# Stick-breaking attention: the break probabilities stay in PSUM and are scanned there

## The chip, the core and the metric

The kernel runs on one core of a Trainium2 chip. The metric is the device time of one execution in microseconds (us). TensorE (PE in the profile) multiplies matrices and writes PSUM, which has eight banks of 128 x 512 fp32 values here; ScalarE (ACT) evaluates functions, VectorE (DVE) does elementwise work and scans, GpSimd (POOL) does elementwise work on SBUF, and SyncE (SP) issues the transfers.

## What is computed

One inference step of a two-layer encoder: 2048 prompt rows and 64 sample rows, each layer with four groups of heads. Group C, which the change touches, is stick-breaking attention, strictly causal, four heads of 64:

```python
z = jnp.einsum('bqhd,bkhd->bhqk', q, k).astype(jnp.float32) * Dh ** -0.5
mask = kpos[None, :] < qpos[:, None]
log_1m = jnp.where(mask, jax.nn.log_sigmoid(-z), 0.0)
tail = lax.cumsum(log_1m, axis=3, reverse=True) - log_1m
w = jnp.where(mask, jnp.exp(jax.nn.log_sigmoid(z) + tail), 0.0)
return jnp.einsum('bhqk,bkhd->bqhd', w.astype(v.dtype), v)
```

So the weight of a key is sigmoid(z) times the product of sigmoid(-z) over all later keys. The kernel works with the products themselves, not with logarithms. Groups A (band attention with a bias), B (latent attention) and M (memory tokens) are softmax attention. A large projection goes into every layer and another comes out of it.

## The kernel before

Two streams of work are written into one program. The projection stream (`p_stream`) multiplies row tiles of 128 by weights that are split into a high and a low part (POOL at line 304, DVE at line 305, tile `wh`) and sums three matmuls for each of eight slices into the PSUM tile `pp` (lines 402, 403, 405). The attention stream (`attention`) walks over units; a unit is up to two query tiles against at most four key tiles. A planner (`target`) chooses after every few instructions which of the two streams goes on. The program that results is then ordered for each engine by a scheduler, which works through the instructions by the place at which they were written and by its own estimate of when their inputs are ready; each engine executes its instructions strictly in that order.

A unit u passes through stages that are spread over several turns of the loop: the scores (`step`, once for each query tile), then `s1b`; a turn later the transposes of its weights (`s2`, PSUM tile `pt`, line 900, with the split into `ph` by ACT at line 903 and DVE at line 136); a turn after that the products with the values (`s3`, line 925). For group C the class is `Stick`. One step: two score matmuls into the PSUM tile `ps` (lines 855, 856), on the diagonal a mask added by DVE (line 1090), sigmoid(-z) by ACT into the SBUF tile `cc` (line 1093), sigmoid(z) by ACT into the SBUF tile `s` (line 1094). In `s1b`, for each of the unit's one or two query tiles: the carry of the later keys is copied (line 1109) or set to one (line 1107), DVE scans `cc` from right to left into `r` (line 1110), and POOL multiplies `s` by `r` (line 1113). A scan's two tensor inputs are both `cc`: the second stands in a minimum that never binds.

The tiles `ps`, `pt` and those of the projection stream's transposes share five PSUM banks (pool `ps_st`). `cc` shares its four SBUF buffers with the keys `kr` of group B; `r` has three buffers, `s` four.

Of the kernel before, what the change touches and what calls it, by code (L numbers as in the profile page):

```python
# [7 lines left out]
F32 = mybir.dt.float32  # L8
F32R = mybir.dt.float32r
BF16 = mybir.dt.bfloat16  # L10
ACTF = mybir.ActivationFunctionType
ALU = mybir.AluOpType
# [52 lines left out]
def hybrid_step(  # L65
# [15 lines left out]
    V, A, G, T = nc.vector, nc.scalar, nc.gpsimd, nc.tensor  # L81
# [5 lines left out]
    def pool(name, bufs=1, **kw):  # L87
        return ctx.enter_context(tc.tile_pool(name=name, bufs=bufs, **kw))

    const = pool("const")  # L90
# [3 lines left out]
    at = pool("at")  # L94
# [22 lines left out]

    mhalf = const.tile([128, 32], F32, name="mhalf")
    V.memset(mhalf, -0.5)

    NQ = 3
    qbuf = [const.tile([128, 2, 256], F32R, name=f"qbuf{i}") for i in range(NQ)]
# [729 lines left out]
    def scores(ps, q, qr, i, kt, kr, c0, n):  # L852
        w = n * 128
        qs = slice(i * 128, (i + 1) * 128)
        T.matmul(ps[:, 0:w], lhsT=q[:, 0, qs], rhs=kt[:, c0:c0 + w], start=True, stop=False)  # L855
        T.matmul(ps[:, 0:w], lhsT=q[:, 1, qs], rhs=kt[:, c0:c0 + w], start=False, stop=(qr is None))  # L856
        if qr is not None:
            T.matmul(ps[:, 0:w], lhsT=qr[:, qs], rhs=kr[:, c0:c0 + w], start=False, stop=True)

    def s_tile():  # L860
        return at.tile([128, 640], F32, tag="s", name="s", bufs=4)
# [87 lines left out]
    class Whole(Unit):  # L949
        def s1a(self):  # L950
            self.sb, self.ps = [], []
            p = self.pair
            for i, (a, e) in enumerate(self.ranges):
                self.sb.append(s_tile())
                for c in sorted({j // 4 for j in range(a, e)}):
                    self.ps.append((i, c))
            self.mx = at.tile([128, 2, 2], F32, tag="mx", name="mx", bufs=4)
            self.k = 0
# [4 lines left out]
        def step(self):  # L963
            p = self.pair
            i, c = self.ps[self.k]
            a, e = self.ranges[i]
            j0, j1 = max(a, 4 * c), min(e, 4 * c + 4)
            w = (j1 - j0) * 128
            ps = ps_st.tile([128, 512], F32, name="ps")
            scores(ps, p["q"], None, i, p["kv"][c][:, 0], None, (j0 - 4 * c) * 128, j1 - j0)  # L970
            o0 = (j0 - a) * 128
            out = self.sb[i][:, o0:o0 + w]
            m = 0 if c == a // 4 else 1
            mx = self.mx[:, i, m:m + 1]
            if self.g == "M":
                V.tensor_scalar(out=out, in0=ps[:, 0:w], scalar1=1.0, scalar2=None, op0=ALU.mult, op1=ALU.max,
                                accum_out=mx)
            else:
                off = j0 * 128 if p["sample"] else 640 - (e - j0) * 128
                V.tensor_tensor_reduce(out=out, in0=ps[:, 0:w], in1=p["bt"][:, off:off + w], scale=1.0,  # L980
                                       scalar=-3e38, op0=ALU.add, op1=ALU.max, accum_out=mx)
            self.k += 1

        def s1b(self):
            p, n = self.pair, self.n
            nm = at.tile([128, 2], F32, tag="nm", name="nm", bufs=6)
            two = [a // 4 != (e - 1) // 4 for a, e in self.ranges]
            V.tensor_scalar(out=nm[:, 0:n], in0=self.mx[:, 0:n, 0], scalar1=-1.0, scalar2=None, op0=ALU.mult)
            if all(two):
                V.scalar_tensor_tensor(out=nm[:, 0:n], in0=self.mx[:, 0:n, 1], scalar=-1.0, in1=nm[:, 0:n],  # L990
                                       op0=ALU.mult, op1=ALU.min)
            else:
                for i in range(n):
                    if two[i]:
                        V.scalar_tensor_tensor(out=nm[:, i:i + 1], in0=self.mx[:, i, 1:2], scalar=-1.0,
                                               in1=nm[:, i:i + 1], op0=ALU.mult, op1=ALU.min)
            for i, (a, e) in enumerate(self.ranges):
                w = (e - a) * 128
                A.activation(out=self.sb[i][:, 0:w], in_=self.sb[i][:, 0:w], func=ACTF.Exp, bias=nm[:, i:i + 1],
                             accum_out=p["rspark"][:, p["qi"][i], p["h"]:p["h"] + 1])  # L1000
# [68 lines left out]

    class Stick(Unit):  # L1070
        def s1a(self):
            self.sb, self.cc, self.k = [], [], 0

        def more(self):
            return self.k < self.n
# [1 line left out]
        def step(self):  # L1077
            p, i = self.pair, self.k
            a, e = self.ranges[i]
            c = a // 4  # L1080
            w = (e - a) * 128
            ps = ps_st.tile([128, 512], F32, name="ps")
            mask = None
            if p["sample"]:
                mask = tri[:, 1]
            elif e == p["ends"][i]:
                mask = tri[:, 0]
            scores(ps, p["q"], None, i, p["kv"][c][:, 0], None, 0, e - a)
            if mask is not None:
                V.tensor_tensor(out=ps[:, w - 128:w], in0=ps[:, w - 128:w], in1=mask, op=ALU.add)  # L1090
            s = s_tile()
            cc = at.tile([128, 512], F32, tag="kr", name="cc", bufs=4)
            A.activation(out=cc[:, 0:w], in_=ps[:, 0:w], func=ACTF.Sigmoid, scale=-0.125)  # L1093
            A.activation(out=s[:, 0:w], in_=ps[:, 0:w], func=ACTF.Sigmoid, scale=0.125)
            self.sb.append(s)
            self.cc.append(cc)
            self.k += 1

        def s1b(self):
            p = self.pair  # L1100
            carry = p.setdefault("carry", [None, None])
            for i, (a, e) in enumerate(self.ranges):
                w = (e - a) * 128
                s, cc = self.sb[i], self.cc[i]
                r = at.tile([128, 513], F32, tag="r", name="r", bufs=3)
                if carry[i] is None:
                    G.memset(r[:, w:w + 1], 1.0)
                else:
                    V.tensor_copy(r[:, w:w + 1], carry[i][:, 0:1])
                V.tensor_tensor_scan(r[:, 0:w][:, ::-1], cc[:, 0:w][:, ::-1], cc[:, 0:w][:, ::-1], r[:, w:w + 1],  # L1110
                                     ALU.mult, ALU.min)
                carry[i] = r
                G.tensor_tensor(out=s[:, 0:w], in0=s[:, 0:w], in1=r[:, 1:w + 1], op=ALU.mult)  # L1113

    def load_kv(d, g, h, c, n, sample):
        kv = at.tile([128, 2, 512], F32R, tag="kv", name="kv", bufs=5)
# [321 lines left out]
    def target(x):  # L1438
        for (x0, y0), (x1, y1) in zip(knots, knots[1:]):
            if x <= x1:  # L1440
                return y0 + (y1 - y0) * (x - x0) / (x1 - x0)
        return knots[-1][1]
# [5 lines left out]
    while gens:  # L1448
# [8 lines left out]
        if len(free) == 2:  # L1457
            s = "a" if at_pos["p"] >= target(at_pos["a"]) else "p"
        else:
            s = free[0]  # L1460
# [110 lines left out]
```

## Time and profile before

| what | value |
|---|---|
| median of 3 runs | 3382.83 us (3377.99 to 3388.35) |
| the profiled execution | 3392.03 us |
| its span, first to last instruction | 3390.2 us |
| PE busy | 3177.9 us, 94% |
| DVE busy | 2728.9 us, 80% |
| ACT busy | 1939.0 us, 57% |
| POOL busy | 1598.4 us, 47% |
| granted TensorE clock, mean | 0.985 |

The profile is one execution seen by the hardware profiler. Each engine has a row of busy time; matmuls are pipelined and overlap, so a busy PE is not a PE at its peak. The idle time before an instruction is put down to the engine whose signal came last. 1.8 us of the profiled execution's time lie outside its span.

### The profile page before, as it was taken

The numbers are of one execution on the slowest core, as the hardware profiler recorded it, in microseconds if no ns is written. First come the engines' busy times: TensorE is split into PE (matmuls) and PEld (weight loads), VectorE is DVE, ScalarE is ACT, GpSimd is POOL, SyncE is SP. The second block draws the span as 40 slices with busy tenths as digits, with TensorE's granted clock in tenths as the row PEclk, the third lists the DMA queues.
The fourth block names the chain that finished last, engine by engine and source line by source line (L and its number), as shares of the span: only waits on it lengthen the run. The fifth ranks groups of instructions, "written<-read, shape, count | busy, mean of one in ns | idle before, by whom it ended". The sixth has DMA issues, their size and how long they took to land. (4 is left out here: it accounts for less than half of the span.)

```text
span 3390.2 us, 75857 instructions
## 1 busy us (share of the span) xinstructions
PE 3177.9 (94%) x24486; PEld 3029.8 (89%) x24486; DVE 2728.9 (80%) x7976; ACT 1939.0 (57%) x5336; POOL 1598.4 (47%) x2353
## 2 busy tenths in 40 slices
PE   8999899899999998999999899988999999999898
PEld 7899899789999988999999788978898998888898
DVE  5686777999788789887778977899878888776994
ACT  4455655567665555566556665656646566654651
POOL 4564455666344256542434635477424454112563
PEclk9999999999999998999999999999999999999999
DMA  6555776435656656565566567634455766556534
GB/s 198 168 147 165 205 203 191 131 101 155 172 155 192 194 165 166 141 191 154 145 186 193 146 177 209 194 111 118 140 142 160 207 193 192 151 149 179 153 110 147
DMA packets 576123, 558.95 MB, mean 165 GB/s; under 512 B 70960, under 2 KB 478000, under 8 KB 575728
## 3 DMA queue, kind: packets, MB, share of 16 engines
q1 hardware_dynamic: 575728, 554.10, 58.3%
q8 instruction: 196, 3.21, 0.4%
q14 instruction: 199, 1.63, 0.2%
HBM read 378.21 MB, written 173.75 MB: 163 GB/s over the span
## 5 line engine op out<-in xcount | busy, mean ns | idle before, releaser
L403 PE MATMUL pp<-wh,xh 128*128 128x256 f32 x4416 | 1268.4, 291 | 33.6 <-DVE wh L305 32.3
L402 PE MATMUL pp<-wh,xh 128*128 128x256 f32 x4416 | 1259.8, 290 | 21.9 <-ACT ev L437 14.4
L405 PE MATMUL pp<-wh,xl 128*128 128x256 f32 (+1 forms) x4416 | 1250.5, 285 | 0.6 <-DVE xl L136 0.4
L403 PEld LDWEIGHTS pp<-wh,xh 128*128 128x128 f32 x4416 | 839.9, 191 | 64.0 <-DVE wh L305 51.3
L402 PEld LDWEIGHTS pp<-wh,xh 128*128 128x128 f32 x4416 | 837.5, 191 | 39.2 <-ACT ev L437 18.5
L405 PEld LDWEIGHTS pp<-wh,xl 128*128 128x128 f32 x4416 | 845.1, 192 | 9.3 <-DVE xl L136 0.8
L304 POOL TENSOR_SCALAR wh<-raw,gc 128x256 fp32r<-128x256 f32 (+1 forms) x848 | 500.1, 604 | 301.6 <-PE pp L405 146.3
L925 PE MATMUL ot<-ph,kv 128*128 128x256 f32 (+1 forms) x3104 | 591.8, 294 | 34.3 <-DVE ph L136 18.8
L903 ACT CAST ph<-pt 128x512 fp32r<-128x512 f32 (+2 forms) x840 | 451.0, 551 | 259.6 <-PE pt L900 231.0
L136 DVE TENSOR_TENSOR ph<-pt,ph 128x512 fp32r<-128x512 f32 (+2 forms) x840 | 525.9, 634 | 68.7 <-ACT ph L903 64.8
L900 PE MATMUL pt<-identr,s 128*128 128x128 f32 x3056 | 509.7, 277 | 25.2 <-POOL s L1113 8.0
L925 PEld LDWEIGHTS ot<-ph,kv 128*128 128x128 f32 x3104 | 458.7, 191 | 56.5 <-DVE ph L136 28.0
L1113 POOL TENSOR_TENSOR s<-s,r 128x512 f32<-128x512 f32 (+3 forms) x328 | 359.6, 1102 | 311.4 <-DVE r L1110 136.9
L305 DVE SCALAR_TENSOR_TENSOR wh<-raw,gc,wh 128x256 fp32r<-128x256 f32 (+1 forms) x848 | 472.5, 582 | 25.0 <-POOL wh L304 22.9
L1110 DVE TENSOR_TENSOR_SCAN r<-cc,r 128x512 f32<-128x512 f32 (+3 forms) x328 | 406.5, 1250 | 15.9 <-ACT cc L1093 14.4
L139 POOL TENSOR_TENSOR st<-st,mhalf 128x4 f32<-128x4 f32 (+1 forms) x312 | 283.3, 913 | 270.9 <-DVE st L463 240.4
L855 PE MATMUL ps<-kv,qbuf 128*128 128x512 f32 (+3 forms) x1024 | 376.7, 371 | 25.7 <-DVE ph L136 5.4
L900 PEld LDWEIGHTS pt<-identr,s 128*128 128x128 f32 x3056 | 361.8, 141 | 43.6 <-POOL s L1113 12.4
L856 PE MATMUL ps<-kv,qbuf 128*128 128x512 f32 (+3 forms) x1024 | 351.1, 345 | 0.0
L437 ACT ACTIVATE ev<-pp,xst 128x256 f32<-128x256 f32 (+1 forms) x424 | 199.9, 473 | 161.7 <-PE pp L405 118.4
L1093 ACT ACTIVATE cc<-ps 128x512 f32<-128x512 f32 (+3 forms) x328 | 178.2, 544 | 192.5 <-DVE ps L1090 153.7
L1051 ACT ACTIVATE s<-s,nm 128x512 f32<-128x512 f32 (+3 forms) x328 | 212.6, 651 | 107.2 <-DVE nm L1043 74.3
(171 smaller groups left out, 5128.9 us busy)
## 6 DMA issues: line engine op xcount, KB each, us to landing
raw<-in_w_in SPq DMA_DIRECT2D x288, 256.0 KB, 3.5
kv<-kvC SPq DMA_DIRECT2D x128, 256.0 KB, 4.3
kv<-kvB SPq DMA_DIRECT2D x128, 256.0 KB, 4.4
kv<-kvA SPq DMA_DIRECT2D x96, 256.0 KB, 4.5
raw<-in_w_out SPq DMA_DIRECT2D x96, 256.0 KB, 3.4
y<-y SPq DMA_DIRECT2D x136, 128.0 KB, 2.5
xin<-y SPq DMA_DIRECT2D x64, 256.0 KB, 3.5
qC<-kt SPq DMA_DIRECT2D x34, 256.0 KB, 3.0
```

What stands on the lines that cost most here:

```text
L136: (eng or V).tensor_tensor(out=dst, in0=src, in1=hi.bitcast(F32), op=ALU.subtract)
L304: G.tensor_scalar(out=h, in0=raw, scalar1=gc[:, k:k + 1], scalar2=1.0, op0=ALU.mult, op1=ALU.mult)
L305: V.scalar_tensor_tensor(out=lo, in0=raw, scalar=gc[:, k:k + 1], in1=h.bitcast(F32), op0=ALU.mult, op1=ALU.subtract)
L402: T.matmul(pp, lhsT=xh[:, k], rhs=wh, start=(k == 0), stop=False)
L403: T.matmul(pp, lhsT=xh[:, k], rhs=wl, start=False, stop=end)
L405: T.matmul(pp[:, 0:w], lhsT=xl[:, k], rhs=wh, start=False, stop=(k == 7))
L855: T.matmul(ps[:, 0:w], lhsT=q[:, 0, qs], rhs=kt[:, c0:c0 + w], start=True, stop=False)
L900: T.transpose(pt[:, (u + x) * 128:(u + x + 1) * 128], self.p_of(i, j), ident)
L903: A.copy(out=ph[:, 0:w], in_=pt[:, 0:w])
L925: T.matmul(ot[:, e * lo, il[0]:il[0] + n], lhsT=p["vt"](j), rhs=phl[:, e, u * 128:(u + n) * 128], start=start and e == 0, stop=stop and e ...
L1110: V.tensor_tensor_scan(r[:, 0:w][:, ::-1], cc[:, 0:w][:, ::-1], cc[:, 0:w][:, ::-1], r[:, w:w + 1], ALU.mult, ALU.min)
L1113: G.tensor_tensor(out=s[:, 0:w], in0=s[:, 0:w], in1=r[:, 1:w + 1], op=ALU.mult)
```

## The change

Each step of `Stick` now does everything for its query tile. sigmoid(z) goes first, into `s`. Then sigmoid(-z) is written by ACT over its own input, the scores in the PSUM bank `ps`; the SBUF tile `cc` is gone. The carry, the scan and POOL's product follow at once in the written order, and `s1b` is empty. The scan reads `ps` in PSUM as its first input; its second is a single column of ones in SBUF, read over and over. The bank `ps` can therefore be used again only when the scan has ended, and not when both sigmoids have.

```diff
+    one = const.tile([128, 1], F32, name="one")
+    V.memset(one, 1.0)
...
             s = s_tile()
-            cc = at.tile([128, 512], F32, tag="kr", name="cc", bufs=4)
-            A.activation(out=cc[:, 0:w], in_=ps[:, 0:w], func=ACTF.Sigmoid, scale=-0.125)
             A.activation(out=s[:, 0:w], in_=ps[:, 0:w], func=ACTF.Sigmoid, scale=0.125)
+
+            cc = ps[:, 0:w]
+            A.activation(out=cc, in_=cc, func=ACTF.Sigmoid, scale=-0.125)
+            carry = p.setdefault("carry", [None, None])
+            r = at.tile([128, 513], F32, tag="r", name="r", bufs=3)
+            if carry[i] is None:
+                G.memset(r[:, w:w + 1], 1.0)
+            else:
+                V.tensor_copy(r[:, w:w + 1], carry[i][:, 0:1])
+            V.tensor_tensor_scan(r[:, 0:w][:, ::-1], cc[:, ::-1], one.to_broadcast([128, w]), r[:, w:w + 1], ALU.mult, ALU.min)
+            carry[i] = r
+            G.tensor_tensor(out=s[:, 0:w], in0=s[:, 0:w], in1=r[:, 1:w + 1], op=ALU.mult)
             self.sb.append(s)
-            self.cc.append(cc)
             self.k += 1

         def s1b(self):
-            p = self.pair
-            carry = p.setdefault("carry", [None, None])
-            for i, (a, e) in enumerate(self.ranges):
-                ...
-                V.tensor_tensor_scan(r[:, 0:w][:, ::-1], cc[:, 0:w][:, ::-1], cc[:, 0:w][:, ::-1], r[:, w:w + 1],
-                                     ALU.mult, ALU.min)
-                carry[i] = r
-                G.tensor_tensor(out=s[:, 0:w], in0=s[:, 0:w], in1=r[:, 1:w + 1], op=ALU.mult)
+            pass
```

First place: ACT in the last stretch of group C, two units of two query tiles each. Line 1093 is sigmoid(-z), line 1094 sigmoid(z). Before:

```order
4011 L1093 ACTIVATE cc<-ps 128x512
4012 L1094 ACTIVATE s<-ps 128x512
4013 L1093 ACTIVATE cc<-ps 128x512
4014 L1094 ACTIVATE s<-ps 128x512
4015 L903 CAST ph<-pt 128x512 x2
```

Now, where line 1094 is sigmoid(z) and line 1097 sigmoid(-z) in place:

```order
4017 L1094 ACTIVATE s<-ps 128x512
4018 L1097 ACTIVATE ps<-ps 128x512
4019 L1094 ACTIVATE s<-ps 128x512
4020 L1097 ACTIVATE ps<-ps 128x512
4021 L905 CAST ph<-pt 128x512 x2
```

The input of the scan is made by the second activation of each pair and no longer by the first.

Second place: DVE at the same point of the program, before. Line 1110 is the scan (it is listed by its instruction's kind), line 1109 the copy of the carry, lines 933 and 947 end the unit in front, line 838 belongs to the output projection, line 1339 to the merge of a group.

```order
6635 L933 TENSOR_TENSOR os<-ot,os 128x256
6636 L947 TENSOR_TENSOR opark<-ob,opark 128x2x64
6637 L1110 SCALAR_TENSOR_TENSOR r<-cc,r 128x512
6638 L1109 COPY r<-r 128x1
6639 L1110 SCALAR_TENSOR_TENSOR r<-cc,r 128x512
6640 L838 TENSOR_TENSOR xr<-pp,xr 128x256
6641 L1339 TENSOR_REDUCE mst<-y 128x4
```

Now (line 1104 is the scan, line 1103 the copy, line 840 what was line 838):

```order
6674 L935 TENSOR_TENSOR os<-ot,os 128x256
6675 L949 TENSOR_TENSOR opark<-ob,opark 128x2x64
6676 L1104 SCALAR_TENSOR_TENSOR r<-ps,r,one 128x512
6677 L840 TENSOR_TENSOR xr<-pp,xr 128x256
6678 L1103 COPY r<-r 128x1
6679 L1104 SCALAR_TENSOR_TENSOR r<-ps,r,one 128x512
6680 L1337 TENSOR_REDUCE mst<-y 128x4
```

One instruction of the projection has moved between the two scans; otherwise the sequence is the same. Over the whole program 71 of the 328 scans stood directly behind another scan (or with a copy of a carry between them), and 55 do now.

## Rows read from the trace of the kernel before

**Rows 1.** The page: busy time, share of the span and instructions of each engine.

```profile
PE 3177.9 (94%) x24486; PEld 3029.8 (89%) x24486; DVE 2728.9 (80%) x7976; ACT 1939.0 (57%) x5336; POOL 1598.4 (47%) x2353
```

**Rows 2.** Busy us (instructions) by stretch: five of group C; last, everything else.

```profile
605.00:810.00 205.00, 184.84 (x1410) 172.51 (x1409) 195.15 (x369) 133.58 (x321) 142.32 (x169) 1.00 0.42 117
3114.00:3300.00 186.00, 169.79 (x1271) 158.79 (x1270) 178.40 (x319) 110.92 (x244) 111.62 (x129) 0.98 0.49 134
sum 896.00, PE 803.92 PEld 750.50 DVE 849.11 ACT 547.42 POOL 589.91; mean PE 160.78 PEld 150.10 DVE 169.82 ACT 109.48 POOL 117.98
...
156.00:273.00 117.00, 113.36 (x915) 110.28 (x914) 98.08 (x209) 63.77 (x169) 81.03 (x121) 0.99 0.58 154
sum 2495.00, PE 2374.02 PEld 2279.29 DVE 1879.78 ACT 1391.55 POOL 1008.46; mean PE 395.67 PEld 379.88 DVE 313.30 ACT 231.92 POOL 168.08
```

**Rows 3.** Groups by shape: line, engine, operation, count | busy us, mean ns | idle us, releasers.

```profile
L1110 DVE TENSOR_TENSOR_SCAN r<-cc,r 128x512 f32<-128x512 f32 x224 | 327.1, 1470 | 6.8 <-ACT cc L1093 6.4 <-issue 0.2
L1113 POOL TENSOR_TENSOR s<-s,r 128x512 f32<-128x512 f32 x224 | 279.4, 1253 | 189.3 <-DVE r L1110 68.2 <-ACT s L1094 27.0 <-ACT ph L903 12.6
```

**Rows 4.** Timeline from 3117.9, DVE, then ACT, POOL, PE: start us, us, instruction.

```profile
3118.80 1.28 DVE L1110 TENSOR_TENSOR_SCAN r<-cc,r 128x512 f32<-128x512 f32 x1 [0.29 <-ACT cc L1093]
3120.19 0.15 DVE L1109 COPY r<-r 128x1 f32<-128x1 f32 x1
3120.26 2.17 DVE L1110 TENSOR_TENSOR_SCAN r<-cc,r 128x512 f32<-128x512 f32 x1
3118.17 0.60 ACT L1093 ACTIVATE cc<-ps 128x512 f32<-128x512 f32 x1
3118.66 0.59 ACT L1094 ACTIVATE s<-ps 128x512 f32<-128x512 f32 x1
3119.14 0.60 ACT L1093 ACTIVATE cc<-ps 128x512 f32<-128x512 f32 x1
3119.61 0.62 ACT L1094 ACTIVATE s<-ps 128x512 f32<-128x512 f32 x1
3120.25 1.09 POOL L1113 TENSOR_TENSOR s<-s,r 128x512 f32<-128x512 f32 x1 [3.03 <-ACT s L1094]
3117.97 0.39 PE L855 MATMUL ps<-kv,qbuf 128*128 128x512 f32 x1
```

**Rows 5.** One line's instructions: count, duration ns min/median/max; the scan, then two others.

```profile
L1110 DVE TENSOR_TENSOR_SCAN r<-cc,r x328: 453/1271/2183, 156.2 to 3299.1; 128x512 f32<-128x512 f32 x100, 128x128 f32<-128x128 f32 x28, 128x384 f32<-128x384 f32 x28, 128x256 f32<-128x256 f32 x8
  ACT cc L1093: 14.4, 24
L501 DVE SCALAR_TENSOR_TENSOR kt<-ptk,qg,kt x102: 448/473/485, 112.0 to 2862.7; 128x256 fp32r<-128x256 f32 x102
L305 DVE SCALAR_TENSOR_TENSOR wh<-raw,gc,wh x848: 351/484/1408, 8.1 to 3373.0; 128x256 fp32r<-128x256 f32 x159, 128x160 fp32r<-128x160 f32 x11
```

**Rows 6.** Line 305 alone in the five stretches of group C: DVE busy us (instructions).

```profile
605.00:810.00 205.00, 25.01 (x40) 1.00 0.42 117
1231.00:1452.00 221.00, 40.64 (x56) 0.95 0.54 148
1853.00:1939.00 86.00, 9.32 (x16) 0.96 0.54 155
2204.00:2402.00 198.00, 23.83 (x35) 0.98 0.39 109
3114.00:3300.00 186.00, 19.78 (x32) 0.98 0.49 134
sum 896.00, DVE 118.59; mean DVE 23.72
```

**Rows 7.** What PE waited for in 605 to 810: us, times, longest.

```profile
PE ps L855 <- DVE kt L501: 2.8, 3, 1.6
PE pt L900 <- POOL s L1113: 2.5, 2, 1.8
PE ps L855 <- DVE xl L136: 0.4, 1, 0.4
PE ps L855 <- DVE ph L136: 0.3, 1, 0.3
```

**Rows 8.** The scan alone in the first, short stretch of group C: DVE busy us (instructions).

```profile
156.00:273.00 117.00, 31.35 (x32) 0.99 0.58 154
```

More of the change, by code (lines that the diff above doesn't have):

```diff
@@ L1071, in s1a @@
         def s1a(self):
-            self.sb, self.cc, self.k = [], [], 0
+            self.sb, self.k = [], 0
         def more(self):
@@ L1091, in step @@
             s = s_tile()
-            cc = at.tile([128, 512], F32, tag="kr", name="cc", bufs=4)
-            A.activation(out=cc[:, 0:w], in_=ps[:, 0:w], func=ACTF.Sigmoid, scale=-0.125)
             A.activation(out=s[:, 0:w], in_=ps[:, 0:w], func=ACTF.Sigmoid, scale=0.125)
+            cc = ps[:, 0:w]
[9 more added lines that the diff above has]
+            G.tensor_tensor(out=s[:, 0:w], in0=s[:, 0:w], in1=r[:, 1:w + 1], op=ALU.mult)
             self.sb.append(s)
-            self.cc.append(cc)
             self.k += 1
         def s1b(self):
-            p = self.pair
-            carry = p.setdefault("carry", [None, None])
-            for i, (a, e) in enumerate(self.ranges):
[L1103 to L1109, printed above, removed]
-                V.tensor_tensor_scan(r[:, 0:w][:, ::-1], cc[:, 0:w][:, ::-1], cc[:, 0:w][:, ::-1], r[:, w:w + 1],
-                                     ALU.mult, ALU.min)
-                carry[i] = r
-                G.tensor_tensor(out=s[:, 0:w], in0=s[:, 0:w], in1=r[:, 1:w + 1], op=ALU.mult)
+            pass
     def load_kv(d, g, h, c, n, sample):
```

## The prediction

> **What bounds the kernel now.** I read the page's first part, then the busy time by stretch, then the scan and what stands round it. Over the whole span PE is the bound: 94% busy, DVE 80% [rows 1]. The reader is to see that this mean hides two regimes. Outside five stretches PE works 2374 of 2495 us (95%) and DVE 1880 (75%). In the five stretches where group C runs, 896 us in all, DVE works 849 us (95%) and PE 804 (90%) [rows 2]. So a quarter of the span is DVE's, and there a microsecond taken off DVE can come off the clock. The first stretch of C, 156 to 273, is not of that kind: PE 113 of 117 us, DVE 98 [rows 2]. It holds 32 of the 328 scans [rows 5, 8]; 296 lie in the five.
>
> The scan is the largest thing that the change touches on DVE: 224 of full width take 327 us, 1470 ns each [rows 3]. That mean is not its own pace. At 3118.80 one takes 1.28 us; the next, started at 3120.26, takes 2.17, and at 3120.25 POOL had begun a product of 1.09 us [rows 4]. The difference, 0.89 us, is most of that product: the scan stood still while POOL held something that it needed. Since the product of one step is released by its scan, it starts just as the scan of the other step does. The median of all scans, 1271 ns, against a maximum of 2183 says that this happens to a minority [rows 5]. POOL pays as well: its product takes 1.09 us alone and 1253 ns in the mean [rows 3, 4].
>
> Who is stopped this way? Line 305 reads two SBUF tensors and takes 484 ns in the middle and up to 1408; line 501, the same operation and width but with its first tensor in PSUM, takes 448 to 485, all 102 times [rows 5]. So the collision falls on instructions with two tensors in SBUF. The scan has two now (`cc` twice) and one after the change.
>
> **The change part by part.**
> *Scan without collision.* 224 x (1.470 - 1.28) = 42.6 us of DVE; of these 296/328 lie in the five stretches: 38 us. The 104 narrower ones I leave out. The column of ones is still an SBUF tensor, but line 501 has one too. Bounds: 0 if a second input of any kind from SBUF can be stopped (line 501 speaks against it), 42.6 if the first stretch gives as well.
>
> *A scan that reads PSUM.* No scan of before does. Line 501 against 305 prices the place of the first input: 473 against 484 ns in the median, so nothing; the spread of line 501, 37 ns, times 328 gives 12 us either way as bounds. I take 0. [...]
>
> *POOL set free.* 224 x (1.253 - 1.09) = 36 us off POOL, which works 590 of 896 us there and hides it [rows 2]. It may still matter through line 305: 179 of these in the five stretches take 118.6 us [rows 6], 663 ns each, where line 501 needs 473: 34 us of collision. POOL can now work while a scan runs, so less of its work meets line 305; but its products and its own half of the split still do. Bounds 0 and 34; I take 5, nearer to 0 because none of these instructions changes.
>
> *sigmoid(-z) second.* The scan's input now starts where sigmoid(z) did, 0.49 us later (3118.17 to 3118.66 [rows 4]). That costs only where DVE waits for it or would begin to. 24 scans waited for it, 14.4 us in all [rows 5]: 24 x 0.49 = 12 us is the low end. The far end is 257 scans that stand behind no other scan (328 less the 71 of the order of before): 126 us. DVE idles only 47 us in the five stretches, so there is nearly always work ahead of a scan: I take 15. If the new order put scans earlier in DVE's queue this would be larger, but it does not: around 3118 the same rows stand in the same order, with one instruction of the projection now between the two scans, and fewer scans stand back to back (55 for 71). ACT's amount of work is as before; writing the result to PSUM instead of SBUF has no row here, and ACT works 547 of 896 us, so it is covered from either side.
>
> *The bank held longer.* The second scores of the pair begin at 3117.97; their bank is released by the end of sigmoid(z), 3120.23, after 2.3 us. With the change it is released by the end of the scan: 3120.26 + 1.28, after 3.6 us [rows 4]. A step comes every 896/296 = 3.0 us, so the scores hold 0.75 banks of the five before and 1.2 after, in the mean. PE's waits in this pool are small now: some 6 us in 205 [rows 7], the line for POOL's product among them. I take 5 us in the five stretches; bounds 0 and 65 (each of 296 steps a sixth of the 1.3 us of longer hold).
>
> *The rest.* The SBUF buffers that `cc` shared with `kr`, the empty `s1b`, one memset at the start: nothing, since neither the loads nor their count change and the memset lies in the first microseconds.
>
> Sum on DVE: -38 - 5 = -43 us. With 95% DVE and 90% PE in those stretches not all of it reaches the clock; I count 0.85 of it, between DVE's share and what is left when PE's own dense pieces are set aside (a choice): -37. Plus 15 plus 5: -17 us. Against the profiled execution, 3392.0 (1.8 of it outside the span), that is 3375. The median of the runs is 3382.8, 9.2 below the profiled one, so on the scale of the runs: 3366 us.
>
> **The rivals.**
> *Full relief.* The scan goes down to 1.28, line 305 is freed too (20 of its 34 us), and the later sigmoid is always covered: -38 - 20 = -58, about 3325. For it: DVE at 95%. Against: line 305 meets POOL's own half of the same split, which stays. Chance 0.10.
> *Nothing to measure.* The later sigmoid takes what the scan gives: from 67 to 85 scans that begin 0.49 us later (33 to 42 us), the time lies within a few us of 3383. For it: the scan at 3118.80 started 0.03 us after its sigmoid, and DVE had waited 0.29. Against: the 24 waits in 328. With it goes the case that the broadcast column collides as `cc` did. Chance 0.20.
> *A scan slower from PSUM*, at the bound of line 501's spread or beyond: 12 us or more off the gain, so 3376 to 3384. [...]
> *Slower: five banks are too few.* The order gives a bank to its next user while the scan still runs; PE, which executes in order, stands in front of that user with all the projection's matmuls behind it, so the DVE queue runs dry a moment later. At a full wait of 1.3 us it wipes out the gain from 28 steps on (37/1.3); at 50 of the 296 it costs 65 us: 65 - 37 + 15 = +43, 3426 at worst and around 3405 at 35 steps. For it: the hold grows by more than half, and DVE at 95% returns banks late. Against: 1.2 banks of five, and PE waits of a few us now. Chance 0.15.
>
> **How the numbers follow.** The forecast, faster by 10 to 45 us, has 0.50 and by itself the range 3338 to 3373; then 0.10 for full relief, 0.20 and 0.05 for nothing to measure, 0.15 for slower. About 0.3%, 10 us here, is what a measurement of this kernel can tell from no change (its three runs lie within 10.4 us). Faster 0.60, same 0.25, slower 0.15. The range for 8 in 10 runs from 3332, inside full relief, to 3402, inside the slower case; it takes in the bounds of the PSUM source and most of those of the later sigmoid.
>
> **What would show it.** Right: the group of 224 scans at about 1.28 us and no scan over 1.4; POOL's product nearer to 1.1; the five stretches some 15 to 45 us shorter in sum, the rest unchanged; DVE's idle time before scans, put down to ACT, up from 14 to about 30 us. Wrong: scans that still reach 2 us (the collision remains); the free scan at 1.34 or more (PSUM costs); idle time before scans over 50 us (the later sigmoid); PE waits of tens of us put down to `r` in front of lines 857 or 902 (the banks). If the stretches outside group C change by more than 10 us, the new order as a whole did something that this working has not priced.

## The result

The changed kernel takes 3336.81 us in the median of four runs (3334.74 to 3338.43), the kernel before 3380.41 beside it: ratio 0.9865, 95% interval 0.985 to 0.988. That is 44 us faster. Forecast were 17: the direction holds and the collision is gone as forecast, the size does not hold, and the time lies near the fast end of the range.

**The profile after.** First the page's busy row, the answer to [rows 1], then the first two of the five stretches of group C, cut at their first and last scan, the sum of the five, and C's first, short stretch, all of the changed kernel (us from and to, length; busy us of PE, PE's weight loads, DVE, ACT, POOL with their instructions; clock, DMA share, GB/s):

```profile
PE 3155.7 (95%) x24486; PEld 3012.4 (90%) x24486; DVE 2658.4 (80%) x7977; ACT 1942.9 (58%) x5336; POOL 1509.3 (45%) x2353
```

```profile
603.20:797.80 194.60, 182.73 (x1406) 171.58 (x1404) 183.81 (x370) 135.17 (x318) 124.59 (x170) 1.00 0.43 121
1224.10:1432.00 207.90, 194.19 (x1487) 183.66 (x1486) 190.76 (x374) 122.27 (x269) 120.53 (x167) 0.98 0.56 158
...
sum 844.40, PE 790.05 PEld 739.36 DVE 789.58 ACT 552.00 POOL 511.05; mean PE 158.01 PEld 147.87 DVE 157.92 ACT 110.40 POOL 102.21
...
154.40:266.30 111.90, 109.79 (x903) 107.37 (x902) 93.66 (x208) 62.43 (x166) 73.07 (x122) 1.00 0.58 162
```

The same cut of the kernel before, its second stretch and the sum:

```profile
1231.90:1451.20 219.30, 200.41 (x1479) 188.35 (x1478) 203.11 (x370) 118.12 (x264) 135.95 (x166) 0.95 0.53 147
...
sum 890.80, PE 800.41 PEld 747.21 DVE 845.60 ACT 542.95 POOL 587.03; mean PE 160.08 PEld 149.44 DVE 169.12 ACT 108.59 POOL 117.41
```

The five stretches are 46.4 us shorter. The profiled span fell by 53.9 (3390.2 to 3336.3), the first short stretch of C by 4.6 (from 156.2-272.7 to 154.4-266.3), and everything else by 2.9. In the five stretches DVE is busy 56.0 us less and idle 9.6 us more (45.2 before, 54.8 after): 56.0 - 9.6 = 46.4. By this account the gain is DVE's, less some new waiting. The profiled execution of the kernel before lay 12 us above the median that stands beside the result, that of the changed kernel 2, so the profiles show 10 us more than the 44 of the medians.

A second thing comes with it, which the prediction had no term for. In the five stretches the granted TensorE clock was 1.00, 0.95, 0.96, 0.98 and 0.98 of full speed before, and 1.00, 0.98, 1.00, 1.00 and 0.98 after. The traces of both kernels have two levels of it, 1.00 and 0.50 of full speed; by these shares TensorE spent some 44 us of the stretches at the lower level before and some 15 after (an estimate: twice the missing share times the length). One such piece of the kernel before, the wait of PE from the timeline and then the cut in which the clock stood at half:

```profile
1321.14 1.01 PE L925 MATMUL ot<-ph,kv 128*128 128x256 f32 x3 [2.93 <-DVE r L1109]
1320.20:1327.00 6.80, 5.27 (x19) 4.38 (x19) 6.80 (x10) 2.91 (x7) 3.82 (x5) 0.50 0.57 154
```

PE had stood still for 2.93 us for a copy of the carry on a DVE that was busy throughout, and the clock fell during that wait (1.00 from 1318 to 1320, 0.50 from 1320.20 on). So part of DVE's relief may reach the time by way of PE's clock; no run here separates that part.

The scan and its neighbours, the answer to [rows 3, 5] (groups: count | busy us, mean ns | idle before; then the scan's min/median/max in ns and what DVE waited for before it):

```profile
L1104 DVE TENSOR_TENSOR_SCAN r<-ps,r,one 128x512 f32<-128x512 f32 x224 | 283.4, 1273 | 16.4 <-ACT ps L1097 15.8
L1106 POOL TENSOR_TENSOR s<-s,r 128x512 f32<-128x512 f32 x224 | 254.8, 1138 | 201.7 <-DVE r L1104 176.8 <-DVE r L1103 5.5 <-DVE st L465 5.0
```

```profile
L1104 DVE TENSOR_TENSOR_SCAN r<-ps,r,one x328: 445/1270/1284, 154.4 to 3245.5; 128x512 f32<-128x512 f32 x100, 128x128 f32<-128x128 f32 x28, 128x384 f32<-128x384 f32 x28, 128x256 f32<-128x256 f32 x8
...
  ACT ps L1097: 28.4, 59
```

No scan takes longer than 1284 ns, where the longest took 2183. The place of [rows 4] in the timeline of the changed kernel (DVE, ACT, POOL; start us, us):

```profile
3074.76 1.28 DVE L1104 TENSOR_TENSOR_SCAN r<-ps,r,one 128x512 f32<-128x512 f32 x1 [0.78 <-ACT ps L1097]
3075.96 0.40 DVE L840 TENSOR_TENSOR xr<-pp,xr 128x256 f32<-128x256 f32 x1
3076.28 0.15 DVE L1103 COPY r<-r 128x1 f32<-128x1 f32 x1
3076.34 1.27 DVE L1104 TENSOR_TENSOR_SCAN r<-ps,r,one 128x512 f32<-128x512 f32 x1
3073.64 0.60 ACT L1094 ACTIVATE s<-ps 128x512 f32<-128x512 f32 x1
3074.14 0.59 ACT L1097 ACTIVATE ps<-ps 128x512 f32<-128x512 f32 x1
3076.13 1.09 POOL L1106 TENSOR_TENSOR s<-s,r 128x512 f32<-128x512 f32 x1 [2.94 <-DVE r L1104]
```

Both sides of the change are to be seen in it. POOL's product runs from 3076.13 and the second scan beside it takes 1.27 us, not 2.17. And the first scan waits 0.78 us for its activation, which comes second now; before it waited 0.29.

### The profile page after: what moved, and what is told of

The parts are those of the page before. It is cut to its first block, busy times and chain, and to the rows that moved or that the text cites. A ratio compares the mean times of both kernels' runs of the same rounds, so it can differ in the third digit from the quotient of the medians.

```text
span 3336.3 us, 75730 instructions
## 1 busy us (share of the span) xinstructions
PE 3155.7 (95%) x24486; PEld 3012.4 (90%) x24486; DVE 2658.4 (80%) x7977; ACT 1942.9 (58%) x5336; POOL 1509.3 (45%) x2353
## 4 chain that ended last, share of the span: by engine, by line
PE 55%; DVE 18%; DMA 13%; issue 5%; ACT 4%; POOL 3%; SPq 2%; POOLq 0%; ACTq 0%; DVEq 0%
PE pp L405 10%; PE pp L404 10%; PE pp L407 9%; PE ot L927 6%; PE pt L902 6%; DVE wh L307 5%; DVE r L1104 3%; PE ps L857 3%; PE ps L858 3%; DVE ph L138 3%; PE ps L860 2%; PE ob L943 1%; DMA y<-y 1%; PE ptx L261 1%; PE ptk L496 1%
## 5 line engine op out<-in xcount | busy, mean ns | idle before, releaser
L306 POOL TENSOR_SCALAR wh<-raw,gc 128x256 fp32r<-128x256 f32 (+1 forms) x848 | 470.4, 570 | 323.8 <-PE pp L407 160.2
L1106 POOL TENSOR_TENSOR s<-s,r 128x512 f32<-128x512 f32 (+3 forms) x328 | 323.9, 988 | 343.0 <-DVE r L1104 293.6
L857 PE MATMUL ps<-kv,qbuf 128*128 128x512 f32 (+3 forms) x1024 | 377.2, 371 | 25.5 <-DVE r L1104 13.1
L1104 DVE TENSOR_TENSOR_SCAN r<-ps,r,one 128x512 f32<-128x512 f32 (+3 forms) x328 | 360.0, 1104 | 30.8 <-ACT ps L1097 28.4
L1094 ACT ACTIVATE s<-ps 128x512 f32<-128x512 f32 (+3 forms) x328 | 175.1, 534 | 145.7 <-DVE ps L1092 93.8
```

The costliest lines, as they stand in the source:

```text
L306: G.tensor_scalar(out=h, in0=raw, scalar1=gc[:, k:k + 1], scalar2=1.0, op0=ALU.mult, op1=ALU.mult)
L1104: V.tensor_tensor_scan(r[:, 0:w][:, ::-1], cc[:, ::-1], one.to_broadcast([128, w]), r[:, w:w + 1], ALU.mult, ALU.min)
```

## The experiments

Each time stands beside the kernel before on the same chip. My theory was the collision: a scan with two tensors in SBUF and POOL's reads of SBUF stop each other (with the change the full scans went from 1470 to 1273 ns in the mean, POOL's full products from 1253 to 1138).

**Order alone, and the data alone.** From the changed kernel, the probabilities back to SBUF; and from the kernel before, the probabilities in place in PSUM, which puts sigmoid(-z) second there too.

```diff
# e1_order_only, from the changed kernel
-            cc = ps[:, 0:w]
-            A.activation(out=cc, in_=cc, func=ACTF.Sigmoid, scale=-0.125)
+            cc = at.tile([128, 512], F32, tag="kr", name="cc", bufs=4)[:, 0:w]
+            A.activation(out=cc, in_=ps[:, 0:w], func=ACTF.Sigmoid, scale=-0.125)
...
-            V.tensor_tensor_scan(..., cc[:, ::-1], one.to_broadcast([128, w]), ...)
+            V.tensor_tensor_scan(..., cc[:, ::-1], cc[:, ::-1], ...)
# e2_psum_old_order, from the kernel before: s1b and its place stay
+    one = const.tile([128, 1], F32, name="one")
+    V.memset(one, 1.0)
...
-            cc = at.tile([128, 512], F32, tag="kr", name="cc", bufs=4)
+            A.activation(out=s[:, 0:w], in_=ps[:, 0:w], func=ACTF.Sigmoid, scale=0.125)
+            cc = ps
             A.activation(out=cc[:, 0:w], in_=ps[:, 0:w], func=ACTF.Sigmoid, scale=-0.125)
-            A.activation(out=s[:, 0:w], in_=ps[:, 0:w], func=ACTF.Sigmoid, scale=0.125)
...
-                V.tensor_tensor_scan(..., cc[:, 0:w][:, ::-1], cc[:, 0:w][:, ::-1], ...)
+                V.tensor_tensor_scan(..., cc[:, 0:w][:, ::-1], one.to_broadcast([128, w]), ...)
```

> The changed kernel's written order (sigmoid(z) first, scan and product beside the scores), but sigmoid(-z) goes to an SBUF tile again and is both inputs of the scan. Theory (collision: the gain comes from the scan having only one tensor in SBUF): the 224 full scans stay near 1470 ns in the mean with a maximum above 2 us, and the time is that of before, 3370 to 3390 us. Rival (order: the gain comes from scan and product standing beside the scores): 3330 to 3345 us.

> Before's written order (scan and product in s1b), but sigmoid(-z) written in place into PSUM and scanned there against the column of ones. Theory (collision): full scans at 1.27 us, time 3330 to 3350 us, as the changed kernel or a little later, since the bank is held longer still. Rival (order): 3370 to 3390 us. Rival (banks: the longer hold costs, and issuing the scan early is what makes it bearable): above 3355 us although the scans take 1.27 us.

Measured: the order alone 3394.3 us against 3384.0, ratio 1.0031 (1.0017 to 1.0046), so slower; the data alone 3342.9, ratio 0.9892 (0.9875 to 0.9908). The full scans, with the order alone and then with the data alone:

```profile
L1104 DVE TENSOR_TENSOR_SCAN r<-cc,r 128x512 f32<-128x512 f32 x224 | 331.8, 1490 | 11.9 <-ACT cc L1097 9.6 <-POOL wh L306 1.2 <-issue 0.5
```

```profile
L1112 DVE TENSOR_TENSOR_SCAN r<-ps,r,one 128x512 f32<-128x512 f32 x224 | 283.5, 1273 | 17.1 <-ACT ps L1096 16.7
```

The written place of scan and product has no part in the gain. More than that: on DVE, ACT and POOL the second kernel has the issue order of the changed kernel but for three instructions on DVE. The scheduler puts scan and product where their inputs are ready, wherever they are written; that half of the change does nothing.

**What collides.** The kernel before (e3), where only the scan's second input becomes the column of ones in SBUF:

```diff
+    one = const.tile([128, 1], F32, name="one")
+    V.memset(one, 1.0)
...
-                V.tensor_tensor_scan(..., cc[:, 0:w][:, ::-1], cc[:, 0:w][:, ::-1], ...)
+                V.tensor_tensor_scan(..., cc[:, 0:w][:, ::-1], one.to_broadcast([128, w]), ...)
```

> Before with one edit: the scan's second input is the column of ones in SBUF, its first stays the SBUF tile cc. Theory (collision counts tensors in SBUF, whatever their width in memory): scans still reach above 2 us, mean of the full ones near 1470 ns, time 3370 to 3390 us. Rival (the collision comes from reading the full tile twice): full scans at 1.27 us and 3330 to 3350 us.

3381.8 us, ratio 0.9992 (0.9979 to 1.0005): no change, and the scans are where they were:

```profile
L1112 DVE TENSOR_TENSOR_SCAN r<-cc,r,one 128x512 f32<-128x512 f32 x224 | 326.8, 1469 | 7.1 <-ACT cc L1095 6.7 <-ACT s L1096 0.3
```

A single column read over and over collides as a full tile does (1469 ns in the mean for 1470, and up to 2186 for 2183). What helped in e2 is that the first input has left SBUF (1273 ns).

**The later sigmoid.** The kernel before with its two activations exchanged (e4):

```diff
+            A.activation(out=s[:, 0:w], in_=ps[:, 0:w], func=ACTF.Sigmoid, scale=0.125)
             A.activation(out=cc[:, 0:w], in_=ps[:, 0:w], func=ACTF.Sigmoid, scale=-0.125)
-            A.activation(out=s[:, 0:w], in_=ps[:, 0:w], func=ACTF.Sigmoid, scale=0.125)
```

> Before with one edit: sigmoid(z) first, sigmoid(-z) second, everything else as it was. It prices the term of the prediction that was put at 15 us. Theory now (other work fills the wait): DVE's idle time before scans, put down to ACT, rises from 14 us by about 10 to 15, but the time rises by no more than 5 us, 3378 to 3386 us. Rival (the term was right): 3392 to 3400 us.

3393.0 us, ratio 1.0042 (1.0022 to 1.0061). The new theory missed here, and the size of the prediction's term of 15 us came out: 14 us, between 7 and 21. The order-only kernel, which has the same issue order but for a few rows, says 10. DVE's idle time before scans rose from 14.4 to 25.2 us. In the five stretches, though, the exchange hardly shows (894 us, and 890 in the order-only kernel, for 891), so where the time is lost stays open: the exchange also changes the issue order of the whole program. The size agrees with the term; the place that the term gave it, DVE's waits in the stretches, is not shown.

**Without sigmoid(z).** The weight is the difference of neighbouring products, r[j+1] - r[j]; e5 from the changed kernel, e12 from the kernel before:

```diff
-            A.activation(out=s[:, 0:w], in_=ps[:, 0:w], func=ACTF.Sigmoid, scale=0.125)
...
-            G.tensor_tensor(out=s[:, 0:w], in0=s[:, 0:w], in1=r[:, 1:w + 1], op=ALU.mult)
+            G.tensor_tensor(out=s[:, 0:w], in0=r[:, 1:w + 1], in1=r[:, 0:w], op=ALU.subtract)
```

> The changed kernel without sigmoid(z): the weight is taken as the difference of neighbouring products, r[j+1] - r[j], by the same POOL instruction with subtract, so that each step has one activation, in place, and the scan's input is ready one activation earlier. It tells what the later sigmoid costs in the changed kernel. Theory (it costs there what it costs in the kernel before with its two sigmoids swapped, 10 to 14 us): DVE's idle time before scans falls from 28 to about 15 us, time 3320 to 3332 us. Rival (the changed kernel hides it): 3334 to 3345 us. A third outcome is slower, if the scheduler's new order is worse.

> Before with the difference of neighbours in place of sigmoid(z), but with the probabilities in SBUF and the scan of two SBUF tensors: the collision stays. It tells whether what the difference gives depends on the collision being gone. Theory (separate terms: 23 us in the changed kernel was the later sigmoid, which before does not have, plus little): 3372 to 3384 us, full scans still near 1470 ns. Rival (the difference gives by itself, through less ACT work): 3355 to 3368 us.

e5: 3313.1 us, ratio 0.9798 (0.9779 to 0.9818), 23 us faster than the changed kernel and faster than its theory, rival or third outcome allowed. DVE's idle time before scans fell to 15.3 us, as expected. e12: 3362.6, ratio 0.9937 (0.9917 to 0.9958), 20 us faster than before although its scan's input was first already, and its full scans at 1421 ns still collide. So the rival's time holds: leaving out 328 activations is worth some 20 us whether the scan collides or not, and e5 does not price the later sigmoid. What makes it worth that is not separated: ACT has less to do, but the scan can also start (e5) or the scores' bank is free (e12) one activation earlier, and POOL's instruction no longer waits for sigmoid(z). Collision and difference add: 44 and 20 to 68.

**The banks.** The three PSUM pools of the kernel before hold 2, 5 and 1 banks, eight in all. Four instead of five in the shared pool, for both kernels (e6 from the kernel before, e7 from the changed one):

```diff
-    ps_st = PsumPool(pool("ps_st", bufs=5, space=PS))
+    ps_st = PsumPool(pool("ps_st", bufs=4, space=PS))
```

> Before with four PSUM banks in the shared pool instead of five. With the next run it tells whether the longer hold of the scores' bank is paid for. Both theories: slower than before by 15 to 80 us.

> The changed kernel with four PSUM banks in the shared pool instead of five. Theory (the longer hold is bearable, five banks are enough with room): the loss against the changed kernel is within 15 us of the loss that the kernel before has from the same edit. Rival (five were just enough, the hold counts): it loses at least 30 us more than the kernel before does.

e6: 3460.5 us, ratio 1.0235 (1.0211 to 1.026), and e7: 3434.7, ratio 1.0153 (1.0127 to 1.0178). One bank costs the kernel before 79 us and the changed one 97, 18 more with an uncertainty of about 13: between the two theories. What the change adds, the longer hold and the later sigmoid together, weighs more with four banks: in the changed kernel DVE's idle time before scans, put down to ACT, is 52.6 us there and 28.4 with five. Five banks carry it without turning the gain.

**The price of a microsecond of DVE.** One more DVE instruction per step, first one that nobody waits for, then one in the chain:

```diff
# e8_extra_dve
+            junk = at.tile([128, 4], F32, tag="junk", name="junk", bufs=1)
+            V.tensor_reduce(out=junk, in_=mhalf.unsqueeze(1).to_broadcast([128, 4, 32]), op=ALU.add, axis=AX.X)
# e11_dve_in_chain
+            V.tensor_tensor(out=ps[:, w - 128:w], in0=ps[:, w - 128:w], in1=one.to_broadcast([128, 128]), op=ALU.min)
             carry = p.setdefault("carry", [None, None])
```

> The changed kernel with one more DVE instruction in each of the 328 steps, a reduction of 128 constant values behind the scan that nobody waits for (estimate 0.28 us each, from the 128-wide rows of the trace). It measures what a microsecond of DVE is worth: 92 us of DVE more, 83 of them in the five stretches. Theory now (DVE is the bound there one to one): 70 to 95 us slower than the changed kernel, 3407 to 3432 us. Rival (the factor of the prediction or less, with slack in DVE): 50 us or less, up to 3390 us.

> The changed kernel with one more DVE instruction per step that can't be moved away: a minimum with one over the last 128 columns of the probabilities in PSUM, which changes no value, between the activation and the scan (estimate 0.29 us by the mask's rows, 85 us in the five stretches). In the last run with an extra instruction the scheduler had placed all 328 in the first 300 us, where DVE has room, so it told nothing on the stretches. Theory (DVE is the bound in the five stretches): 50 to 95 us slower than the changed kernel, 3387 to 3432 us. Rival (slack there as well): 3335 to 3365 us.

e8: 3333.9 us, as the changed kernel, although its 328 reductions take 91.2 us on DVE. It answers another question than it was made for: the scheduler put all 328 into the first 300 us, so more DVE work there, outside the five stretches, cost nothing. e11: 3356.9, ratio 0.9924 (0.9896 to 0.9952), 20 us slower. My theory expected 50 or more and missed; the time lies in the rival's range. Its five stretches:

```profile
sum 887.70, PE 828.18 PEld 765.88 DVE 848.03 ACT 556.52 POOL 510.15; mean PE 165.64 PEld 153.18 DVE 169.61 ACT 111.30 POOL 102.03
```

DVE is busy 58 us more, the stretches are 43 us longer, and PE does 38 us more of work in them, which is then not left for later. So the stretches, 95.5% DVE, do grow with DVE's work, but of their 43 us only 20 reach the whole time. That a longer stretch is not all lost when a new order fills it with projection work is my reading of PE's 38 us. The instruction also delays the scan and holds the bank longer, so this is not the price of DVE's work alone.

**The collision alone.** What every kernel so far had together, this one (e13) takes apart: from the kernel before with four banks, the fifth bank holds the column of ones. Nothing is held longer, sigmoid(-z) stays first, and the issue order is that of e6 but for a few rows.

```diff
-    ps_st = PsumPool(pool("ps_st", bufs=5, space=PS))
+    ps_st = PsumPool(pool("ps_st", bufs=4, space=PS))
...
+    ps_1 = PsumPool(pool("ps_1", bufs=1, space=PS))
...
+    one = ps_1.tile([128, 1], F32, name="one")
+    V.memset(one, 1.0)
...
-                V.tensor_tensor_scan(..., cc[:, 0:w][:, ::-1], cc[:, 0:w][:, ::-1], ...)
+                V.tensor_tensor_scan(..., cc[:, 0:w][:, ::-1], one.to_broadcast([128, w]), ...)
```

> Before with four banks in the shared pool, as in the run e6, and the fifth bank given to the column of ones: the scan reads cc from SBUF and the ones from PSUM. One tensor in SBUF, no longer hold of the scores' bank, sigmoid(-z) still first, and the issue order of e6 but for a few rows. Against e6 (3460 us) it prices the collision alone. Theory (the collision is the whole gain, and the later sigmoid and the longer hold took little of it): 40 to 65 us faster than e6, 3395 to 3420 us, full scans at 1.27 us. Rival (the collision alone gives what the prediction counted, 37 us or less, and the rest of the gain came from the new order): 3423 us and more.

3404.4 us, ratio 1.0060 (1.0047 to 1.0073). Against e6, 1.0235 - 1.0060 = 0.0175 of 3382 us: 59 us, give or take 9 (the plain medians differ by 56, the two profiled spans by 48). The full scans, e6 first, then this kernel:

```profile
L1110 DVE TENSOR_TENSOR_SCAN r<-cc,r 128x512 f32<-128x512 f32 x224 | 329.0, 1477 | 10.2 <-ACT cc L1093 9.3
```

```profile
L1113 DVE TENSOR_TENSOR_SCAN r<-cc,r,one 128x512 f32<-128x512 f32 x224 | 282.6, 1270 | 15.3 <-ACT cc L1096 14.1
```

The five stretches in sum, in the same order:

```profile
sum 899.30, PE 806.92 PEld 749.02 DVE 849.89 ACT 546.06 POOL 581.74; mean PE 161.38 PEld 149.80 DVE 169.98 ACT 109.21 POOL 116.35
```

```profile
sum 846.20, PE 786.88 PEld 736.79 DVE 782.76 ACT 546.29 POOL 500.51; mean PE 157.38 PEld 147.36 DVE 156.55 ACT 109.26 POOL 100.10
```

DVE is busy 67 us less in the five stretches and POOL 81, and the stretches are 53 us shorter. Here too the granted clock is higher, in the third stretch 0.96 for 0.88. The changed kernel with four banks is 31 us slower than this one (1.0153 against 1.0060): that is what the longer hold, the exchanged sigmoids and the new order cost with four banks.

**A faster version.** The high part of the weights' split from POOL to ACT, in the changed kernel alone (e9) and together with the difference (e10):

```diff
-            G.tensor_scalar(out=h, in0=raw, scalar1=gc[:, k:k + 1], scalar2=1.0, op0=ALU.mult, op1=ALU.mult)
+            A.activation(out=h, in_=raw, func=ACTF.Copy, scale=gc[:, k:k + 1])
```

> The changed kernel with the high part of the weights' split (line 306) moved from POOL to ACT, so that POOL no longer reads SBUF for it while DVE subtracts. Theory (collision with POOL stretches every DVE instruction with two SBUF tensors): the low part on DVE falls from 584 to below 540 ns in the mean and in the five stretches the clock gains 5 to 20 us, if ACT has the room: 3315 to 3332 us. Rival (ACT has not: 848 more activations of about 0.5 us lie in front of what PE waits for): 3345 us and more.

> The difference of neighbours (no sigmoid(z)) together with the high part of the split on ACT. Theory: sigmoid(z) gave ACT the room back, so the two add: 3290 to 3310 us. Rival (ACT in front of PE): 3320 us and more.

e9: 3327.6 us, ratio 0.9840 (0.9813 to 0.9866), and e10: 3306.2, ratio 0.9772 (0.9743 to 0.9800). The low part on DVE (line 307) falls from 584 to 518 ns in e9. Alone the step is within its uncertainty of the changed kernel. With the difference it has the lowest time of this study, 31 us below the changed kernel, but it cannot be told from the difference alone (0.9772 against 0.9798, each known to 0.002 or 0.003). So the gain shown is the difference's; that the split adds to it is not shown.

## Why the prediction was wrong in size

*The place.* Right: the five stretches give 46 of 54 us of span. The first stretch was counted at nothing and gave 4.6.

*The scan.* Right in its pace: predicted 1.28 us and none over 1.4, measured 1273 ns and at most 1284; the full scans give 43.7 us of DVE (327.1 less 283.4) for 42.6. In the five stretches all scans give 43.7 us too, where 38 were counted: 212 of the 224 full ones lie there, and the narrower ones, which I left out, had collided as well (128x384 fell from 1061 to 1012 ns).

*A scan from PSUM.* Right at nothing: 1273 ns from PSUM in the changed kernel, and 1.28 us in the kernel before for the scan at 3118.80, which has both inputs in SBUF and was not stopped. No run shows a scan from PSUM at the 1.34 us that was to mean a cost: of 328 in the changed kernel none takes longer than 1284 ns, in e9 1286 at most, and the median is 1270 for 1271 before.

*POOL set free.* This is the first step that failed, a term that was too small: "I take 5, nearer to 0 because none of these instructions changes". In the five stretches DVE is busy 56.0 us less; the scans give 43.7, so 12 came from other instructions, and 17 of 67 in e13 against e6, where the issue order stays. The scans alone in the five stretches, before and changed, then e6 and e13:

```profile
sum 890.80, DVE 374.95; mean DVE 74.99
sum 844.40, DVE 331.25; mean DVE 66.25
sum 899.30, DVE 380.38; mean DVE 76.08
sum 846.20, DVE 330.21; mean DVE 66.04
```

Over the whole span DVE is busy 70.5 us less (2728.9 to 2658.4), of which the scans of all widths are 47 (407.8 to 360.6, summed over the four shapes); some 23 us came from other instructions. Line 305, on which I had looked, gave 5 (591 to 584 ns). The rest came from those that I had not listed. DVE groups of the changed kernel, then the same three of before (lines 627, 476, 138 are lines 625, 474, 136 there); the first two read two SBUF tensors, the third has its first tensor in PSUM:

```profile
L627 DVE SCALAR_TENSOR_TENSOR ev<-sg,ev 128x256 f32<-128x256 f32 x136 | 59.9, 443 | 20.7 <-ACT sg L626 20.2
L476 DVE TENSOR_TENSOR nrm<-ev,st 128x256 f32<-128x256 f32 x106 | 54.3, 513 | 16.2 <-POOL st L141 10.3 <-DMA o_akp<-nrm 2.6 <-PE ptk L496 1.8
L138 DVE TENSOR_TENSOR ph<-pt,ph 128x512 fp32r<-128x512 f32 x616 | 416.2, 681 | 58.8 <-ACT ph L905 55.4
```

```profile
L625 DVE SCALAR_TENSOR_TENSOR ev<-sg,ev 128x256 f32<-128x256 f32 x136 | 68.7, 508 | 20.0 <-ACT sg L624 18.9 <-DMA gM<-ev 0.5
L474 DVE TENSOR_TENSOR nrm<-ev,st 128x256 f32<-128x256 f32 x106 | 58.2, 549 | 17.2 <-POOL st L139 10.0 <-DMA o_akp<-nrm 4.8 <-PE ptk L494 1.4
L136 DVE TENSOR_TENSOR ph<-pt,ph 128x512 fp32r<-128x512 f32 x616 | 415.9, 682 | 58.0 <-ACT ph L903 54.6
```

The mean falls by 65 and 36 ns where both tensors lie in SBUF and stays where one is in PSUM (682 and 681 ns). POOL lost 89 us of busy time, where I had counted 36 for its product alone (the full products gave 25). So POOL meets DVE's other two-tensor instructions less. The five stretches of e6 and e13 hold the same 398 TENSOR_TENSOR and SCALAR_TENSOR_TENSOR instructions without a PSUM input; summed over the trace, POOL is at work during 188 us of them in e6 and 153 in e13. That it is there less because the scans no longer stop it is the reading that fits; it was not tested by itself.

*The factor.* I let 0.85 of DVE's relief reach the clock; with one and the same order, e13 against e6, 53 of 67 us did (0.79) in the stretches. Right, a little high. What the higher TensorE clock gives is inside this number.

*The later sigmoid and the bank.* Here the sum failed a second time. I set 20 us against the gain and lost 6 more by the factor, all of it in the five stretches. There DVE's idle time, which holds both, rose by 9.6 us. DVE's waits before scans did go from 14.4 to 28.4 us, predicted about 30. PE's idle time in front of the scores (line 855, now 857) stayed: 25.7 us before, 25.5 after, 13.1 of it now put down to the scan, so the longer hold hardly shows with five banks.

Whole runs give another view. The exchanged sigmoids cost 14 and 10 us (e4, e1). From e4 to e2, and from e1 to the changed kernel, only the scan's inputs change, the probabilities to PSUM and the second to the column of ones: 51 us, give or take 9, and 56, give or take 7. That is the end of the collision less the longer hold, with five banks, though the scheduler orders the two of a pair differently (some 1730 of DVE's 7977 instructions). Beside the 59 for the collision alone, with four banks, the hold cannot be told from nothing or from the 5 us that I took. The 15 us for the sigmoid thus agree in size with 14 and 10, but where in the program these are lost stays open.

So the sum in the stretches should have read 56 us less of DVE instead of 43, and 9.6 lost on the way to the clock instead of 26. By whole runs it should have read 59 for the collision instead of 37; the 15 left over against it is a remainder, known to about 11, and no measurement of its own. The rival "full relief" had the mechanism for it, but looked for the second part at line 305.

## What to carry to other kernels

When two engines stop each other, count both: the one that is set free is busy for less time (POOL 89 us less here) and, by the reading above, stops third instructions less; those gained a third to a half as much again of DVE's time as the instruction that changed (17 us beside 50, 23 beside 47). Ask of each DVE instruction beside a busy POOL how many of its tensors lie in SBUF, broadcast columns included; for the scan one fewer ended the collision, whichever of its two inputs moved (1470 to 1273 ns with the first, 1477 to 1270 with the second). Where a scheduler orders the program, a move in the written order may change nothing: compare the issue orders before pricing it.

## What the hardware showed that I had not expected

A broadcast column of ones in SBUF collides as a full tile does (1469 ns in the mean against 1470). DVE operations of 128 x 4 values with two SBUF inputs can be stopped too: one of line 1348, whose median is 155 ns, started at 3164.93 in the kernel before and took 1.01 us, until POOL's products, which had run since 3162.99, ended at 3165.93.
